# Adding DMAs for half of the weights' block sums and for the residual, with a third set of Strassen's products per down column pair

## The chip, the cores and the metric

The kernel runs on one core of a Trainium2 chip. The metric is device microseconds of one execution, the median of several runs. The engines named below are TensorE (PE), VectorE (DVE), ScalarE (ACT), GpSimd (POOL) and SyncE (SP); SP issues the loads, POOL issues a few other transfers, and both kinds run on the core's 16 DMA engines.

## The reference

A decoder layer on 256 tokens with a model width of 2048, all in float32: a half-step SwiGLU FFN, a mixer (attention with a sliding window beside a convolution module), and a second half-step FFN, each followed by LayerNorm of `ALPHA * x + sublayer(x)`. The change touches the two FFNs alone:

```python
D_MODEL, SEQ, D_FF = 2048, 256, 5632

def swiglu_ffn(x, w_gate, w_up, w_down):
    h = jax.nn.silu(x @ w_gate) * (x @ w_up)
    return h @ w_down

x = layer_norm(DEEPNORM_ALPHA * x + 0.5 * swiglu_ffn(x, ffn1_w_gate[l], ffn1_w_up[l], ffn1_w_down[l]), ln1_g[l], ln1_b[l])
...
x = layer_norm(DEEPNORM_ALPHA * x + 0.5 * swiglu_ffn(x, ffn2_w_gate[l], ffn2_w_up[l], ffn2_w_down[l]), ln3_g[l], ln3_b[l])
```

## The kernel before

**Numbers in two parts.** Each float32 weight block is split into a high part (a cast on ScalarE, line 153 or 236) and a low part (a subtraction on VectorE, line 157 or 239); so is the activation. A product is three matmuls: high by high, low by high, high by low (`mm3`, lines 624 to 626), each with a 128 x 128 stationary block and 512 moving columns.

**Strassen's sets.** The up and the down projections take their work in sets. A set is two blocks of the contraction by two column blocks of the weights by the two blocks of 128 tokens. A plain set ("C") makes eight products from two loaded pieces of 128 x 1024. A Strassen set ("S") makes seven from the same two pieces: it forms four sums of weight blocks, and on the other side four sums of activation blocks (`block_sums`). Its products 1, 5, 6 and 7 gather in PSUM banks that belong to several outputs; `shared` combines them with VectorE into four tiles `tmp`, after the last S of a pass (`by_sums`, `final`). The other banks are added by `out` when the last set ends. The eight banks fill PSUM, so the next pass can start a bank only when it has been emptied.

**Passes.** An FFN has 5632 hidden units in three parts of 16, 16 and 12 blocks of 128 (`PARTS`). For each part the up projections run in pairs of groups (`pair`), eight sets each in the order of `UP`, two of them S; then the down projection runs (`down_by_sums`), for two pairs of 512-wide column blocks, eight sets each by the string in `KINDS`. The third part has no S in the down projection and runs through `tokens_by`. In `down_by_sums` the four `tmp` tiles are added to the residual `xt` on VectorE (`plus`, line 885), queued in `st.soon`, and the other banks are added by line 881.

**The planner.** `Steps` issues the splits ahead of their use. `sources` lists the pieces in order of use. `load` keeps up to four load slots (`RAW_BUFS`) filled by DMAs of SP; an S takes one slot and one tile `rawx` of a second pool, and at most two S are open. `jobs` holds what is loaded and not yet split; `ahead` and `pace` run jobs while the block is less than seven ahead of the one in use (`LEAD`) and the eight buffers (`RING`) last. `pace` counts the time of a product against an estimated backlog of VectorE. The low part of a job is put off in `pending` until the next job. For an S, `zeroth` splits the first piece, `first` forms two sums (line 171) and splits them, `second` forms and splits a third block, `third` the fourth.

**The turn of the hidden units.** After a pair of groups, `turn` transposes the gated result on VectorE (`hr`, line 963) and sends it through DRAM by POOL: four DMAs `far` (line 968) and one `hf` (line 970), issued at once. Six steps later `split` makes the high and low blocks `hh` and `hl` for the down projection, seven for a set of kind S and four for C. A step is one call of `st.step`: two in each set, one for each piece in `tokens_by`. All engines run their instructions in the order written.

Of the kernel before, what the change touches and what calls it, by code (L numbers as in the profile page):

```python
# [9 lines left out]
F32 = mybir.dt.float32  # L10
# [4 lines left out]
ALU = mybir.AluOpType  # L15
# [3 lines left out]
P = 128  # L19
# [3 lines left out]
KT = D // P  # L23
JT = DFF // P
PARTS = ((0, 16), (16, 32), (32, 44))
KINDS = ("SCCSCCCC", "SCCSCCCC", None)
BLOCKS = {"S": 7, "C": 4}
UP = (
    ((2, "C"), (3, "C"), (0, "S"), (4, "C"), (1, "S"), (5, "C"), (6, "C"), (7, "C")),
# [23 lines left out]
BC = 6  # L53
# [21 lines left out]
class Steps:  # L75
# [6 lines left out]
    def __init__(self, nc, pool, sources, head, pooled, xT, x_raw, xcat):  # L82
        self.nc, self.pool, self.sources, self.head, self.pooled = nc, pool, sources, head, pooled
        self.xT, self.x_raw, self.xcat = xT, x_raw, xcat
        self.loaded = self.open = self.whole = self.done = self.used = self.now = 0
        self.jobs, self.ready, self.pending, self.sets = [], {}, [], 0
        self.later, self.background, self.backlog = [], None, 0.0
        self.paced, self.soon = False, []
        self.most = len(sources)

        n = KT // 2
        self.order = [g * n + t for t in range(TURNS) for g in range(2)]
        self.order += [g * n + t for g in range(2) for t in range(TURNS, n)]
# [13 lines left out]
    def raw(self):  # L107
# [2 lines left out]
        self.open += 1  # L110
        return self.pool.tile([P, 1024], F32, tag="raw", name=f"raw{n}", bufs=RAW_BUFS)

    def load(self):
        while self.open < RAW_BUFS and self.loaded < len(self.sources):
            n = self.loaded
            if isinstance(self.sources[n], tuple):
                if self.sets == 2:
                    return
                self.load_set(n)
                continue  # L120
            if n < 4:

                raws = [self.raw(), self.raw()]
                self.get_x(n, 2)
                for q in range(2):
                    for i in range(2):
                        self.get(raws[i], n + i, q * 512, 512)
                self.jobs += [("free", None, None)] * 2
                continue
            raw = self.raw()  # L130
            if n < len(self.order) and self.order[n] < KT // 2:
                self.get_x(2 * self.order[n], 2)
            self.get(raw, n, 0, 1024)
            self.jobs.append(("free", None, None))

    def load_set(self, n):

        raws = [self.raw(), self.extra.tile([P, 1024], F32, tag="rawx", name=f"rawx{n}", bufs=2)]
        self.sets += 1
        self.loaded += 3  # L140
        for raw, src in zip(raws, self.sources[n][0]):
            self.nc.sync.dma_start(raw, src)
        for i, work in enumerate((self.zeroth, self.first, self.second, self.third)):
            self.jobs.append((n + i, raws, work))

    def upper(self, n, raw):

# [19 lines left out]
            self.pending.pop(0)()  # L167
            most -= 1

    def sub(self, out, a, b):  # L170
        self.nc.vector.tensor_tensor(out=out, in0=a, in1=b, op=ALU.subtract)  # L171
        self.vector(0.6)

    def zeroth(self, n, raws):
        zero = self.upper(n, raws[0])
        self.flush()
        raws.append(zero)

    def first(self, n, raws):
        a, b = ([r[:, :512], r[:, 512:]] for r in raws[:2])  # L180
        t = [self.act.tile([P, 512], F32, tag="bc", name=f"sum{n}", bufs=BC) for _ in range(2)]
        raws.append(t)
        self.sub(t[0], b[0], a[0])
        self.sub(t[1], b[1], t[0])
        self.pending = [raws[2], self.upper(n, t)]

    def second(self, n, raws):
        b = [raws[1][:, :512], raws[1][:, 512:]]
        self.sub(b[0], b[1], b[0])
        self.pending.append(self.upper(n, raws[1]))  # L190
        self.flush(1)

    def third(self, n, raws):
        a1 = raws[0][:, 512:]
        self.sub(a1, a1, raws[3][1])
        three = self.upper(n, a1)
        self.flush(1)

        def ended():
            three()  # L200
            self.open -= 1
            self.sets -= 1
            self.load()

        self.pending.append(ended)

    def split(self):
        nc = self.nc
# [121 lines left out]
def hybrid_layer(  # L330
# [3 lines left out]
    nc = tc.nc  # L334
# [530 lines left out]
    def down_by_sums(hh, hl, kinds, factor):  # L865

        firsts = [sum(BLOCKS[k] for k in kinds[:t]) for t in range(len(kinds))]
        places = {
            "S": ("11", "22", "12", "S1", "S2", "S3", "S4"),
            "C": ("21", "11", "22", "12"),  # L870
        }

        def blocks(t, name):
            n = firsts[t] + places[kinds[t]].index(name)
            return hh[:, n], hl[:, n]

        for c in range(0, NC_, 2):
            ys = {(i, j): xt[:, 1 - i, (c + j) * 512 : (c + j + 1) * 512] for i in range(2) for j in range(2)}

            def add(out, ps, other):  # L880
                nc.vector.scalar_tensor_tensor(out=out, in0=ps, scalar=factor, in1=other, op0=ALU.mult, op1=ALU.add)
                st.vector(0.62, 0.3)

            def plus(y, t):
                nc.vector.tensor_tensor(out=y, in0=y, in1=t, op=ALU.add)
                st.vector(0.6)

            def shared(bank, ys=ys):

                tmp = [act.tile([P, 512], F32, tag="z", name="part", bufs=ZB) for k in range(4)]  # L890
                nc.scalar.mul(tmp[0], bank[1], factor)
                add(tmp[1], bank[6], tmp[0])
                add(tmp[3], bank[5], tmp[1])
                add(ys[1, 1], bank[5], ys[1, 1])
                add(tmp[2], bank[7], tmp[1])
                for n, (at, k) in enumerate((((0, 0), 0), ((0, 1), 3), ((1, 0), 2), ((1, 1), 2))):
                    st.soon.append(lambda y=ys[at], t=tmp[k]: plus(y, t))

            by_sums(kinds, blocks, lambda at, ps, ys=ys: add(ys[at], ps, ys[at]), shared)

    def ffn(xc, tag, skew, begun, prepare, finish, kept=None):
        with tc.tile_pool(name=f"ffn{tag}", bufs=2) as pool:
# [17 lines left out]
            def block_sums(out, x_):  # L920

                for o, y, z, op in (
                    (out[:, 0], x_[0], x_[2], ALU.add), (out[:, 2], x_[1], x_[0], ALU.subtract),
                    (out[:, 1], out[:, 0], x_[1], ALU.subtract), (out[:, 3], x_[3], out[:, 1], ALU.subtract),
                ):
                    nc.vector.tensor_tensor(out=o, in0=y, in1=z, op=op)
                    st.vector(0.2)
# [8 lines left out]
            for part, ((j0, j1), kinds) in enumerate(zip(PARTS, KINDS)):  # L936
                n = j1 - j0
# [22 lines left out]
                def turn(g, ht, hh=hh, hl=hl, kinds=kinds):  # L960
# [3 lines left out]
                    st.vector(1.25)  # L964
                    far = dram.tile([4, 32, 4, 2 * P], F32, tag="far", name="far")

                    for t in range(4):
                        nc.gpsimd.dma_start(far[:, :, t].rearrange("f r n -> r f n"), hr[32 * t : 32 * t + 32])  # L968
                    hf = pool.tile([P, 8 * P], F32, tag="ht", name="hf")
                    nc.gpsimd.dma_start(hf, far.rearrange("f r t n -> (f r) (t n)"))  # L970

                    def parted(at, src):
                        hi, lo = (x_[:, at : at + src.shape[1]] for x_ in (hh, hl))
# [18 lines left out]
                        parted(at, some[:, 1:])  # L992
                        parted(at + 3, sums)

                    st.at(6, lambda: st.soon.extend([lambda t=t: split(hf, t) for t in range(2)]))

                def pair(g, ups):

                    tmp, places = [], {(0, 0): 0, (0, 1): 2, (1, 0): 1, (1, 1): 3}

                    def add(out, ps, other):
                        nc.vector.tensor_tensor(out=out, in0=ps, in1=other, op=ALU.add)  # L1002
                        st.vector(0.62, 0.3)

                    def shared(bank):

                        tmp.extend(act.tile([P, 512], F32, tag="z", name="part", bufs=ZB) for k in range(4))
                        nc.scalar.copy(tmp[0], bank[1])
                        add(tmp[1], bank[6], tmp[0])
                        add(tmp[2], bank[5], tmp[1])  # L1010
                        add(tmp[1], bank[7], tmp[1])
                        add(tmp[3], bank[5], tmp[1])

                    def out(at, ps):

                        y = tmp[places[at]]
                        add(y, ps, y)
                        nc.scalar.activation(y[:, : JG * P], y[:, : JG * P], AF.Silu)

                    def gates():  # L1020
                        for at, k in places.items():
                            gate(g + at[1], 1 - at[0], tmp[k], tmp[k][:, : JG * P])
                        turn((g - j0 // JG) // 2, gated.pop())

                    by_sums("".join(kind for _, kind in ups), lambda n, name: up_blocks(ups[n][0], name), out, shared)
                    st.at(1, gates)
# [471 lines left out]
```

## Time and profile before

| | us |
|---|---|
| median of 3 runs | 1687.98 |
| lowest and highest | 1686.88, 1688.58 |
| the profiled execution | 1688.99 |
| its span | 1687.2 |

The span runs from the first to the last instruction that the profiler records. The profile's groups give count, busy time, the mean of one instruction in ns, and the engine's idle time just before them with what ended most of it. The lines themselves stand in the prediction.

### The profile page before, as it was taken

To read this page: it belongs to the slowest core of one execution; us is meant where nothing else is said; L and a number is where in the kernel's file an instruction comes from. 1 tells how busy PE (TensorE), PEld (TensorE's weight loads), DVE (VectorE), ACT (ScalarE), POOL (GpSimd) and SP (SyncE) were. 2 spreads that over 40 slices of the span, in tenths; PEclk is the share of its full clock that TensorE was granted. 3 is DMA by queue.
4 is the path that set the end of the run, shared out by engine and by line. 5 is a ranking of instruction groups with operands and counts; after the bars stand their busy time and mean duration, and the time that the engine had idled before them with its cause. 6 is when DMAs were issued, how large, how long until landed. Compare 5 with 4: busy or idle time off the path is not lost.

```text
span 1687.2 us, 21755 instructions
## 1 busy us (share of the span) xinstructions
PE 1669.7 (99%) x7689; PEld 1383.6 (82%) x7689; DVE 1386.7 (82%) x2035; ACT 912.9 (54%) x1252; POOL 268.1 (16%) x226
## 2 busy tenths in 40 slices
PE   9999999999999999999999999999999999999997
PEld 7887788888888888888888888877888888888886
DVE  7888898789888886758887778998888888988866
ACT  6556555555555554576665465555545555545541
POOL 0100000000000000178996200000000000000000
PEclk9999999999999999999999999999999999999999
DMA  8767666567666667556654555776656665666682
GB/s 295 241 211 271 219 209 218 191 223 244 214 215 211 212 213 246 171 182 194 200 181 157 198 193 196 246 236 210 219 200 215 221 237 202 222 200 224 209 279 99
DMA packets 103694, 359.47 MB, mean 213 GB/s; under 512 B 12960, under 2 KB 13088, under 8 KB 103328
## 3 DMA queue, kind: packets, MB, share of 16 engines
q1 hardware_dynamic: 96048, 334.74, 58.6%
q0 software_dynamic: 7392, 23.08, 4.5%
q8 instruction: 60, 0.98, 0.2%
q14 instruction: 50, 0.41, 0.1%
q10 hardware_dynamic: 144, 0.26, 0.0%
HBM read 344.40 MB, written 13.63 MB: 212 GB/s over the span
## 4 chain that ended last, share of the span: by engine, by line
PE 67%; DVE 19%; DMA 6%; issue 5%; ACT 3%; DVEq 0%; POOL 0%; ACTq 0%; SPq 0%; POOLq 0%
PE sum L624 13%; PE sum L625 13%; PE sum L626 13%; DVE lo L157 9%; PE acc L624 4%; PE acc L626 4%; PE acc L625 4%; DMA raw<-in_wu 3%; ACT hi L153 2%; DVE part L1002 2%; DVE sum L171 2%; PE in_c L1149 2%; PE in_a L1149 2%; PE in_q L1149 1%; DMA raw<-in_wd 1%
## 5 line engine op out<-in xcount | busy, mean ns | idle before, releaser
L157 DVE TENSOR_TENSOR lo<-raw,hi 128x1024 fp32r<-128x1024 f32 x452 | 506.6, 1153 | 121.5 <-ACT hi L153 121.0
L153 ACT CAST hi<-raw 128x1024 fp32r<-128x1024 f32 x452 | 432.9, 996 | 298.9 <-DMA raw<-in_wu 108.1
L624 PE MATMUL sum<-hi,xcat 128*128 128x512 f32 x1080 | 420.4, 389 | 1.6 <-DVE part L1002 1.6
L625 PE MATMUL sum<-lo,xcat 128*128 128x512 f32 x1080 | 420.3, 389 | 0.6 <-DVE lo L157 0.6
L626 PE MATMUL sum<-hi,xcat 128*128 128x512 f32 x1080 | 420.2, 389 | 0.0
L624 PEld LDWEIGHTS sum<-hi,xcat 128*128 128x128 f32 x1080 | 202.7, 188 | 44.7 <-DVE part L1002 2.5
L625 PEld LDWEIGHTS sum<-lo,xcat 128*128 128x128 f32 x1080 | 202.7, 188 | 42.9 <-DVE lo L157 1.0
L626 PEld LDWEIGHTS sum<-hi,xcat 128*128 128x128 f32 x1080 | 202.7, 188 | 42.2
L968 POOL DMA_DIRECT2D far<-hr x88 | 48.8, 556 | 1167.3 <-DVE hr L963 1120.9
L236 ACT CAST hi<-raw 128x1024 fp32r<-128x1024 f32 (+1 forms) x164 | 166.6, 1030 | 119.9 <-PE acc L626 71.8
L624 PE MATMUL sum<-hi,hh 128*128 128x512 f32 x496 | 194.0, 391 | 1.9 <-DVE part L1002 1.3
L239 POOL TENSOR_TENSOR lo<-raw,hi 128x1024 fp32r<-128x1024 f32 x73 | 175.6, 2423 | 117.5 <-ACT hi L236 110.6
L626 PE MATMUL sum<-hi,hl 128*128 128x512 f32 x496 | 193.1, 389 | 0.0
L625 PE MATMUL sum<-lo,hh 128*128 128x512 f32 x496 | 193.0, 389 | 0.0
L153 ACT CAST hi<-sum 128x512 fp32r<-128x512 f32 x112 | 69.5, 622 | 139.1 <-DVE sum L171 128.9
L239 DVE TENSOR_TENSOR lo<-raw,hi 128x1024 fp32r<-128x1024 f32 (+1 forms) x91 | 106.9, 1203 | 37.9 <-ACT hi L236 37.1
L1002 DVE TENSOR_TENSOR part<-sum,part 128x512 f32<-128x512 f32 x160 | 105.1, 685 | 12.7 <-PE sum L626 8.1
L624 PEld LDWEIGHTS sum<-hi,hh 128*128 128x128 f32 x496 | 93.1, 188 | 25.1 <-DVE part L1002 3.5
L626 PEld LDWEIGHTS sum<-hi,hl 128*128 128x128 f32 x496 | 93.1, 188 | 19.4
L625 PEld LDWEIGHTS sum<-lo,hh 128*128 128x128 f32 x496 | 93.1, 188 | 18.8
L1212 DVE SCALAR_TENSOR_TENSOR conv<-hc,cw_sb,conv 128x256 f32<-128x256 f32 x231 | 96.6, 482 | 1.1
L153 ACT CAST hi<-rawx 128x1024 fp32r<-128x1024 f32 x56 | 59.0, 1053 | 48.9 <-DVE rawx L171 39.3
(198 smaller groups left out, 2319.2 us busy)
## 6 DMA issues: line engine op xcount, KB each, us to landing
raw<-in_wu SPq DMA_DIRECT2D x308, 512.0 KB, 4.8
raw<-in_wd SPq DMA_DIRECT2D x160, 512.0 KB, 4.7
raw<-in_win SPq DMA_DIRECT2D x52, 512.0 KB, 4.1
rawx<-in_wu SPq DMA_DIRECT2D x40, 512.0 KB, 6.3
raw<-in_wout SPq DMA_DIRECT2D x32, 512.0 KB, 3.7
far<-hr POOLq DMA_DIRECT2D x88, 128.0 KB, 2.7
hf<-far POOLq DMA_DIRECT2D x22, 512.0 KB, 3.6
rawx<-in_wd SPq DMA_DIRECT2D x16, 512.0 KB, 6.4
```

The costliest lines, as they stand in the source:

```text
L153: self.nc.scalar.copy(hi, x_)
L157: self.nc.vector.tensor_tensor(out=lo, in0=x_, in1=hi.bitcast(F32), op=ALU.subtract)
L171: self.nc.vector.tensor_tensor(out=out, in0=a, in1=b, op=ALU.subtract)
L236: nc.scalar.copy(hi, raw)
L239: eng.tensor_tensor(out=lo, in0=raw, in1=hi.bitcast(F32), op=ALU.subtract)
L624: nc.tensor.matmul(ps, s_hi, m_hi, start=start, stop=False)
L625: nc.tensor.matmul(ps, s_hi, m_lo, start=False, stop=False)
L626: nc.tensor.matmul(ps, s_lo, m_hi, start=False, stop=stop)
L968: nc.gpsimd.dma_start(far[:, :, t].rearrange("f r n -> r f n"), hr[32 * t : 32 * t + 32])
L1002: nc.vector.tensor_tensor(out=out, in0=ps, in1=other, op=ALU.add)
L1149: nc.tensor.matmul(ps, w[0][:, n], x1[:, k], start=k == 0, stop=False)
L1212: nc.vector.scalar_tensor_tensor(out=out, in0=x_, scalar=w, in1=acc, op0=ALU.mult, op1=ALU.add)
```

## The change

`KINDS` becomes `SCCSCSCC` in two parts of each FFN, so each pass of the down projection has three S. Of the four block sums of an S, VectorE forms two (`sums`, both into tiles of the pool `bc`); the other two are made in place by DMAs that add, issued by POOL. `sums` is put in the list of jobs before the piece that was loaded ahead of the set, and `third` is held until the next piece is loaded. The four `tmp` tiles of the down projection are added to the residual by adding DMAs. Signs are turned so that only additions are needed. The DMAs `far` and `hf` are issued one and three steps after the transpose, and the split follows at step 7 instead of 6.

```diff
-KINDS = ("SCCSCCCC", "SCCSCCCC", None)
+KINDS = ("SCCSCSCC", "SCCSCSCC", None)
...
+    def last_third(self):
+        if self.held is not None:
+            self.jobs.append(self.held)
+            self.held = None
...
     def load_set(self, n):
...
-        for i, work in enumerate((self.zeroth, self.first, self.second, self.third)):
+        early = len(self.jobs) > 3 and self.jobs[-1][0] == "free"
+        at = len(self.jobs) - 2 if early else len(self.jobs)
+        self.jobs.insert(at, (n - early, raws, self.sums))
+        for i, work in enumerate((self.zeroth, self.first, self.second)):
             self.jobs.append((n + i, raws, work))
+        self.held = (n + 3, raws, self.third)
...
+    def sums(self, n, raws):
+        a, b = ([r[:, :512], r[:, 512:]] for r in raws[:2])
+        t = [self.act.tile([P, 512], F32, tag="bc", name=f"sum{n}", bufs=BC) for _ in range(2)]
+        raws.append(t)
+        self.plus(t[0], a[0], b[0])
+        self.plus(t[1], t[0], b[1])
+        self.nc.gpsimd.dma_start(b[0], b[1], accum_op=ALU.add)
 
     def zeroth(self, n, raws):
         zero = self.upper(n, raws[0])
         self.flush()
-        raws.append(zero)
+
+        def ended():
+            zero()
+            self.nc.gpsimd.dma_start(raws[0][:, 512:], raws[2][1], accum_op=ALU.add)
+
+        self.pending = [ended]
 
     def first(self, n, raws):
-        a, b = ([r[:, :512], r[:, 512:]] for r in raws[:2])
-        t = [self.act.tile([P, 512], F32, tag="bc", name=f"sum{n}", bufs=BC) for _ in range(2)]
-        raws.append(t)
-        self.sub(t[0], b[0], a[0])
-        self.sub(t[1], b[1], t[0])
-        self.pending = [raws[2], self.upper(n, t)]
+        one = self.upper(n, raws[2])
+        self.flush()
+        self.pending = [one]
 
     def second(self, n, raws):
-        b = [raws[1][:, :512], raws[1][:, 512:]]
-        self.sub(b[0], b[1], b[0])
-        self.pending.append(self.upper(n, raws[1]))
-        self.flush(1)
+        two = self.upper(n, raws[1])
+        self.flush()
+        self.pending = [two]
 
     def third(self, n, raws):
-        a1 = raws[0][:, 512:]
-        self.sub(a1, a1, raws[3][1])
-        three = self.upper(n, a1)
-        self.flush(1)
+        three = self.upper(n, raws[0][:, 512:])
+        self.flush()
...
                 nc.scalar.mul(tmp[0], bank[1], factor)
                 add(tmp[1], bank[6], tmp[0])
-                add(tmp[3], bank[5], tmp[1])
-                add(ys[1, 1], bank[5], ys[1, 1])
+                add(tmp[3], bank[5], tmp[1], ALU.subtract)
                 add(tmp[2], bank[7], tmp[1])
-                for n, (at, k) in enumerate((((0, 0), 0), ((0, 1), 3), ((1, 0), 2), ((1, 1), 2))):
-                    st.soon.append(lambda y=ys[at], t=tmp[k]: plus(y, t))
+                add(tmp[1], bank[5], tmp[2], ALU.subtract)
+                for at, k in ((0, 0), 0), ((0, 1), 3), ((1, 0), 2), ((1, 1), 1):
+                    nc.gpsimd.dma_start(ys[at], tmp[k], accum_op=ALU.add)
...
-                    for t in range(4):
-                        nc.gpsimd.dma_start(far[:, :, t].rearrange("f r n -> r f n"), hr[32 * t : 32 * t + 32])
+                    def leave():
+                        for t in range(4):
+                            nc.gpsimd.dma_start(far[:, :, t].rearrange("f r n -> r f n"), hr[32 * t : 32 * t + 32])
+
                     hf = pool.tile([P, 8 * P], F32, tag="ht", name="hf")
-                    nc.gpsimd.dma_start(hf, far.rearrange("f r t n -> (f r) (t n)"))
+                    st.at(1, leave, True)
+                    st.at(3, lambda: nc.gpsimd.dma_start(hf, far.rearrange("f r t n -> (f r) (t n)")), True)
...
-                    st.at(6, lambda: st.soon.extend([lambda t=t: split(hf, t) for t in range(2)]))
+                    st.at(7, lambda: st.soon.extend([lambda t=t: split(hf, t) for t in range(2)]))
```

More of the change, by code (lines that the diff above doesn't have):

```diff
@@ L111, in raw @@
         return self.pool.tile([P, 1024], F32, tag="raw", name=f"raw{n}", bufs=RAW_BUFS)
+    def last_third(self):
+        if self.held is not None:
+            self.jobs.append(self.held)
+            self.held = None
     def load(self):
@@ L118, in load @@
                     return
+                self.last_third()
                 self.load_set(n)
@@ L134, in load @@
             self.jobs.append(("free", None, None))
+            self.last_third()
     def load_set(self, n):
@@ L168, in flush, with plus @@
             most -= 1
-    def sub(self, out, a, b):
-        self.nc.vector.tensor_tensor(out=out, in0=a, in1=b, op=ALU.subtract)
+    def plus(self, out, a, b):
+        self.nc.vector.tensor_tensor(out=out, in0=a, in1=b, op=ALU.add)
         self.vector(0.6)
+    def sums(self, n, raws):
[5 more added lines that the diff above has]
+        self.nc.gpsimd.dma_start(b[0], b[1], accum_op=ALU.add)
     def zeroth(self, n, raws):
@@ L878, in down_by_sums, with add @@
             ys = {(i, j): xt[:, 1 - i, (c + j) * 512 : (c + j + 1) * 512] for i in range(2) for j in range(2)}
-            def add(out, ps, other):
-                nc.vector.scalar_tensor_tensor(out=out, in0=ps, scalar=factor, in1=other, op0=ALU.mult, op1=ALU.add)
+            def add(out, ps, other, op=ALU.add):
+                nc.vector.scalar_tensor_tensor(out=out, in0=ps, scalar=factor, in1=other, op0=ALU.mult, op1=op)
                 st.vector(0.62, 0.3)
-            def plus(y, t):
-                nc.vector.tensor_tensor(out=y, in0=y, in1=t, op=ALU.add)
-                st.vector(0.6)
             def shared(bank, ys=ys):
@@ L922, in block_sums @@
                 for o, y, z, op in (
-                    (out[:, 0], x_[0], x_[2], ALU.add), (out[:, 2], x_[1], x_[0], ALU.subtract),
-                    (out[:, 1], out[:, 0], x_[1], ALU.subtract), (out[:, 3], x_[3], out[:, 1], ALU.subtract),
+                    (out[:, 0], x_[0], x_[2], ALU.subtract), (out[:, 2], x_[1], x_[0], ALU.subtract),
+                    (out[:, 1], out[:, 0], x_[1], ALU.subtract), (out[:, 3], x_[3], out[:, 1], ALU.add),
                 ):
@@ L993, in split, with add @@
                         parted(at + 3, sums)
-                    st.at(6, lambda: st.soon.extend([lambda t=t: split(hf, t) for t in range(2)]))
+                    st.at(7, lambda: st.soon.extend([lambda t=t: split(hf, t) for t in range(2)]))
                 def pair(g, ups):
                     tmp, places = [], {(0, 0): 0, (0, 1): 2, (1, 0): 1, (1, 1): 3}
-                    def add(out, ps, other):
-                        nc.vector.tensor_tensor(out=out, in0=ps, in1=other, op=ALU.add)
+                    def add(out, ps, other, op=ALU.add):
+                        nc.vector.tensor_tensor(out=out, in0=ps, in1=other, op=op)
                         st.vector(0.62, 0.3)
@@ L1009, in shared @@
                         add(tmp[1], bank[6], tmp[0])
-                        add(tmp[2], bank[5], tmp[1])
+                        add(tmp[2], bank[5], tmp[1], ALU.subtract)
                         add(tmp[1], bank[7], tmp[1])
-                        add(tmp[3], bank[5], tmp[1])
+                        add(tmp[3], bank[5], tmp[1], ALU.subtract)
                     def out(at, ps):
```

2 lines of the change are left out of this document (1 added, 1 removed).

## The prediction

> **What bounds the kernel now.** I read the page's head and its chain of waits first, then the busy time of TensorE in stretches, then TensorE's timeline row by row, then VectorE's groups with the shapes kept apart, and last the transfers.
>
> ```profile
> span 1687.2 us, 21755 instructions
> PE 1669.7 (99%) x7689; PEld 1383.6 (82%) x7689; DVE 1386.7 (82%) x2035; ACT 912.9 (54%) x1252; POOL 268.1 (16%) x226
> PE 67%; DVE 19%; DMA 6%; issue 5%; ACT 3%; DVEq 0%; POOL 0%; ACTq 0%; SPq 0%; POOLq 0%
> ```
>
> TensorE is all but full, VectorE has about a fifth free, and the chain still runs through VectorE for 19% of the span: weights are sometimes ready only just in time. A busy TensorE need not be at its peak pace, so I count its matmuls in stretches (columns: stretch, length, busy time with count, clock, DMA share, GB/s) and look at single starts (start, duration).
>
> ```profile
> 100.00:200.00 100.00, 98.55 (x431) 1.00 0.68 237
> 200.00:300.00 100.00, 99.87 (x441) 1.00 0.63 213
> 300.00:400.00 100.00, 100.00 (x443) 1.00 0.66 222
> 1000.00:1100.00 100.00, 99.42 (x439) 1.00 0.63 217
> 1100.00:1200.00 100.00, 97.72 (x425) 1.00 0.67 226
> ```
>
> ```profile
> 121.32 0.39 PE L624 MATMUL sum<-hi,xcat 128*128 128x512 f32 x1
> ...
> 134.24 0.39 PE L624 MATMUL sum<-hi,xs 128*128 128x512 f32 x1
> ...
> 1101.67 0.39 PE L626 MATMUL sum<-hi,xs 128*128 128x512 f32 x1
> 1102.95 0.50 PE L624 MATMUL sum<-hi,xcat 128*128 128x512 f32 x1 [0.89 <-DVE part L1002]
> ```
>
> From 121.32 to 134.24 lie 19 products of three matmuls: 12.92 / 57 = 0.227 us from start to start. The 389 ns shown for one matmul overlap its neighbours and are not what one costs. At this pace 100 us hold 443, as in 300 to 400. The other four stretches lack 12, 2, 4 and 18, so 36 starts or 8.2 us are lost there, although three of them look 98 to 100% busy. The pair at 1101.67 shows how: the next start comes 1.28 us later instead of 0.23, since VectorE's adds (L1002) had not yet emptied the bank. Ahead of such a place in FFN 1 the chain reads (start, length):
>
> ```profile
> 152.04 4.13 DMA raw<-in_wu
> ...
> 161.32 6.95 DMA rawx<-in_wd
> ...
> 179.87 2.40 DVE part L1002 x4
> ```
>
> Late transfers made VectorE late, and VectorE is too full to catch up at once.
>
> **The products.** Each FFN has two parts with Strassen's products in the down projection, each runs two column pairs: 8 passes. Each pass gets one more set S (7 products) for a set C (8). That is 8 products or 24 matmuls, 24 x 0.227 = **5.4 us** less on the engine that is full. The same two 512 KB blocks are loaded by S and by C, so no weight traffic is added. The Trainium skill (TensorE: Matmul & The Clock Gate, Back-to-back issue gap) gives about 131 ns as the sustained spacing of such matmuls, by which 24 would be 3.1 us; this trace has 0.227 us, and that decides.
>
> **VectorE.**
>
> ```profile
> L157 DVE TENSOR_TENSOR lo<-raw,hi 128x1024 fp32r<-128x1024 f32 x396 | 470.9, 1219 | 112.3 <-ACT hi L153 111.7
> L1002 DVE TENSOR_TENSOR part<-sum,part 128x512 f32<-128x512 f32 x160 | 105.1, 685 | 12.7 <-PE sum L626 8.1 <-ACT part L1008 2.0
> L157 DVE TENSOR_TENSOR lo<-sum,hi 128x512 fp32r<-128x512 f32 x112 | 72.0, 683 | 0.0
> L171 DVE TENSOR_TENSOR sum<-rawx,sum 128x512 f32<-128x512 f32 x56 | 38.8, 692 | 1.9
> L171 DVE TENSOR_TENSOR raw<-raw,sum 128x512 f32<-128x512 f32 x56 | 38.4, 685 | 0.8
> L157 DVE TENSOR_TENSOR lo<-raw,hi 128x512 fp32r<-128x512 f32 x56 | 38.3, 685 | 9.3 <-ACT hi L153 9.3
> L171 DVE TENSOR_TENSOR rawx<-rawx 128x512 f32<-128x512 f32 x56 | 38.3, 684 | 0.0
> L171 DVE TENSOR_TENSOR sum<-rawx,raw 128x512 f32<-128x512 f32 x56 | 37.8, 675 | 11.7 <-DMA rawx<-in_wd 7.1 <-DMA rawx<-in_wu 4.5
> L949 DVE TENSOR_TENSOR ht<-part 128x256 f32<-128x256 f32 x80 | 28.5, 417 | 0.0
> L963 DVE STREAM_TRANSPOSE hr<-ht 128x1024 f32<-128x1024 f32 x22 | 27.4, 1245 | 0.7
> L885 DVE TENSOR_TENSOR xt<-xt,part 128x512 f32<-128x512 f32 x32 | 19.9, 682 | 0.0
> ```
>
> Two of a set's four block sums go to DMAs: 56 x (0.684 + 0.685) = 76.7 us. The 32 additions to the residual (L885) go too: 32 x 0.682 = 21.8. An S cost VectorE four sums (2.74), two wide lows (2.44) and three narrow ones (2.05), 7.22 us; with two sums it is 5.86. A C costs 2.44. Eight added sets bring 8 x 3.42 = 27.4 us, and the four added splits of the hidden units into seven blocks an estimated 4 x 2.5 = 10 (four small sums and one more low, at 0.69 for 512 columns, with a start for each). Net about 61 us of 1386.7 go.
>
> By stage: an up pair is 186 matmuls or 42.2 us of TensorE. VectorE's share of it was 2 x 7.22 + 6 x 2.44 + 8 x 0.685 + 4 x 0.417 + 1.25 + about 1.4 of splits = 38.9, and becomes 36.2. A down pair had 2 x 7.22 + 6 x 2.44 + 12 adds of 0.68 = 37.2 of 42.2, and gets 3 x 5.86 + 5 x 2.44 + 8 x 0.68 = 35.2 of 41.5. So about 6 us are free in either. ScalarE gets twelve wide casts more in all and is 54% busy: nothing.
>
> What is the relief worth? Between nothing and the 8.2 us lost above. Those stretches start with transfers, which the change makes more of, so I take a quarter: **2 us**.
>
> **The adding DMAs.** No row shows one. There are 2 x 64 for sets and 8 x 4 for the residual, 160 of 256 KB. The nearest rows (issue to landing in us) and the waits for the sets' second half:
>
> ```profile
> far<-hr POOLq DMA_DIRECT2D x88, 128.0 KB, 2.7
> hf<-far POOLq DMA_DIRECT2D x22, 512.0 KB, 3.6
> rawx<-in_wd SPq DMA_DIRECT2D x16, 512.0 KB, 6.4
> L968 POOL DMA_DIRECT2D far<-hr x88: 550/551/747, 55.9 to 1617.0; - x88
> q0 software_dynamic: 7392, 23.08, 4.5%
> DVE sum L171 <- DMA rawx<-in_wd: 7.1, 6, 1.4
> DVE sum L171 <- DMA rawx<-in_wu: 4.5, 7, 1.2
> ```
>
> Landing lies between 2.7 and 6.4; I take 3.6, since reading source and target moves 512 KB. POOL spends 160 x 0.55 = 88 us on issues in stages where it is idle. On the engines 41.9 MB at q0's rate are 8%, twice that if the target counts again, over the share of 0.63 to 0.68 in the stretches above.
>
> **The waits this adds.** (1) The third block's DMA starts after the first sum. ScalarE's cast of that block stops all casts behind it until it lands, then its low stops VectorE. Between the first sum and this low VectorE has 0.69 + 3 lows of 1.22, 1.22 and 1.37 = 4.5 us to do; with landing L the block's high is ready at L + 1.05. So VectorE loses L - 3.5 a set: 0.1 at 3.6, nothing against 6 us free. (2) The sums stand up to two lows (2.44 us) earlier in VectorE's queue, so VectorE, and the lows behind, may wait for the 6.4 us landing of rawx. It waited 13 times in 56 before. At most 2.44 a set: 4.9 of 6 free in an up pair, 7.3 of 6.3 in a down pair, so 0 to 8 us; I take 0, as the weights run up to seven blocks ahead. The load slot of a set is also held one block longer; the same lead covers it, and without it each such load is one 2.4 us job late. (3) The last adds of a pass wait for the residual's DMAs. From `shared` to the first of them are 12 products, 8.2 us; the four tmp adds take 2.7, the scaling 0.6, an issue 0.55 and landing 3.6: 7.5, so hidden. If late, the bank is next needed 8 products (5.4 us) on. (4) `far` and `hf` are issued some steps later, so POOL's queue is free for the adding DMAs instead of waiting on a transpose. Their reader moves from step 6 to 7. In the up stages steps of 2.4 us or more remain. In the last part of FFN 2 it is close:
>
> ```profile
> 1628.56 1.14 ACT L976 CAST hh<-hf 128x512 fp32r<-128x512 f32 x2 [1.57 <-DMA hf<-far]
> 1629.21 1.29 DVE L977 TENSOR_TENSOR hl<-hf,hh 128x512 fp32r<-128x512 f32 x2 [0.96 <-ACT hh L976]
> 1631.62 0.39 PE L624 MATMUL acc<-hi,hh 128*128 128x512 f32 x1
> ```
>
> The first half is ready at 1629.9 and needed at 1631.6; one more cast and low (1.0 and 1.2 us) ahead of it cost 0 to 1.2 us. I take **0.3**.
>
> **Sum.** -5.4 - 2.0 + 0.3 = -7.1. The profiled execution took 1688.99 us, 1.8 more than its span; 1681.9 would follow, and as the median of the runs shown is 1.0 lower, **1680.9**.
>
> **Rivals.** *All the relief*: VectorE, 3 to 6% freer in each stage, is never late. For: the late adds are its own. Against: transfers start the lateness. -5.4 - 8.2 gives 1674.4. *New waits eat it*: wait (2) in full, 8 us in the down pairs, with the products' 5.4: 1690.6; at half, 1686.6. For: VectorE already waited for rawx. Against: all weights run ahead. *Slower*: landing of the adding DMAs. The point is where a down pair's three waits pass its 6.3 us: 3 x (L - 3.5) = 6.3, L = 5.6. At the 6.4 of rawx, 3 x 2.9 - 6.3 = 2.4 us in each of 8 pairs, 19 - 5.4 = +14: 1702. For: those are loads of like traffic. Against: POOL's own queue shows 2.7 and 3.6. *Starved issues*: POOL, writing the descriptors, waits out two wide lows of VectorE at each issue, 2.4 us; that is L = 6.0 and by the same count 3 x 2.5 - 6.3 = 1.2 in each of 8 pairs, 10 - 5.4 = +4.6: 1692.6. Against: 88 issues beside such lows took 550 to 747 ns. The Trainium skill (SBUF — State Buffer, SBUF: two separate sides) says that a VectorE operation holding the ports shared with GpSimd keeps it from writing descriptors, 3100 ns instead of 620; by that rule the slow issues would be seen here, and the trace of before does not show them.
>
> **How the numbers follow.** Forecast and its neighbours (1677 to 1684) 0.50; all the relief 0.14; new waits 0.22, mostly inside 0.2%; slower by landing 0.11; starved issues 0.03. A measurement of this kernel tells 0.2% or 3.4 us from no change. Faster takes the first two and 0.02 of the third: 0.66; same 0.18; slower 0.02 + 0.14 = 0.16. The range 1675 to 1689 leaves out the slower cases and the tip of the relief, under 0.2.
>
> **What would show it.** Right: TensorE at 443 in each stretch of 100 us, 24 matmuls fewer; L885 gone; L171 two to a set; adding DMAs landing under 5 us; 61 us less VectorE. Wrong: TensorE waits on lows or on the last adds in the down pairs; idle before the casts put down to an adding DMA; long waits of the sums for rawx.

## The result, and the profile after

The changed kernel takes 1809.51 us (median of 4 runs, 1808.03 to 1811.1) against 1688.28 us before: a ratio of 1.0718, with a 95% interval of 1.0699 to 1.0736. It is slower by 121 us, where 1680.9 us was forecast.

The head of the page of the changed kernel, and its chain of waits:

```profile
span 1806.7 us, 22167 instructions
PE 1708.4 (95%) x7665; PEld 1395.4 (77%) x7665; DVE 1333.8 (74%) x1951; ACT 917.9 (51%) x1280; POOL 410.2 (23%) x386
PE 40%; DMA 27%; DVE 18%; issue 7%; ACT 4%; POOL 2%; SPq 1%; DVEq 0%; ACTq 0%; POOLq 0%
```

TensorE runs 24 matmuls fewer (7665 instead of 7689), and VectorE has 53 us less to do, as it should be. Still the span is 119.5 us longer. TensorE's idle time, span less busy time, went from 17.5 to 98.3 us: 80.8 us. Its busy time grew by 38.7 us although there is less work: after each wait a matmul stands alone in the record with 0.39 us or more instead of the 0.227 that it costs in a full row, and some ran at a lower clock. The chain went from 6% on transfers to 27%.

The stretches of TensorE (length, busy time with count, granted clock, DMA share, GB/s), first by 100 us and then inside one of the worst:

```profile
200.00:300.00 100.00, 87.68 (x361) 0.92 0.83 231
300.00:400.00 100.00, 100.00 (x434) 0.98 0.76 225
500.00:600.00 100.00, 87.27 (x357) 0.93 0.79 219
```

```profile
220.00:240.00 20.00, 18.97 (x82) 1.00 0.81 223
240.00:260.00 20.00, 14.47 (x48) 0.74 0.87 244
260.00:280.00 20.00, 20.00 (x90) 1.00 0.66 198
```

200 to 300 and 500 to 600 are for the most part down projections of FFN 1. They start 361 and 357 matmuls where a full stretch has 443. The second fence shows where slower matmuls come from: from 240 to 260 TensorE is granted 0.74 of its clock, so 48 matmuls in 14.47 busy us take 0.30 us each, not 0.227. Inside it the clock falls to 0.50 after a wait, so there the wait is paid a second time in slow matmuls. Here are that place and another, each with the start of the matmul that waited (in brackets how long) and a short stretch behind it:

```profile
241.72 0.50 PE L643 MATMUL sum<-hi,hh 128*128 128x512 f32 x1 [2.26 <-DVE xt L900]
244.00:246.00 2.00, 0.77 (x2) 0.50 1.00 311
1220.27 0.50 PE L643 MATMUL sum<-hi,hh 128*128 128x512 f32 x1 [3.20 <-DVE part L1020]
1220.00:1222.00 2.00, 1.65 (x6) 1.00 0.97 358
```

The Trainium skill (TensorE: Matmul & The Clock Gate, HAM oscillation — how this bites in real kernels) states that gaps of more than about 3.4 us throttle the clock. In this trace the clock also fell behind a wait of 2.26 us, and it stayed at 1.00 behind one of 3.20 us, so the length of one wait does not decide it alone.

Who waited for whom in the changed kernel (us in total, times, longest):

```profile
ACT hi L165 <- DMA raw<-sum: 214.0, 58, 7.8
ACT hi L165 <- DMA rawx<-rawx: 142.2, 60, 7.4
DVE sum L183 <- DMA rawx<-in_wu: 55.1, 27, 5.1
DVE sum L183 <- DMA rawx<-in_wd: 27.2, 13, 5.2
PE sum L643 <- DVE xt L900: 49.5, 22, 4.6
DVE xt L900 <- DMA xt<-part: 36.7, 16, 4.4
```

Nearly every set (58 and 60 of 64) makes ScalarE wait twice, for the fourth block's sum (`raw<-sum`, 3.7 us each) and for the third's (`rawx<-rawx`, 2.4 us). The sums on VectorE wait for their load 40 times in 64; before it was 13 in 56. One set in the timeline, ScalarE's rows and then POOL's (start, duration, in brackets the idle time ahead and what ended it):

```profile
329.57 1.05 ACT L165 CAST hi<-rawx 128x1024 fp32r<-128x1024 f32 x1 [2.74 <-DMA rawx<-rawx]
330.52 1.05 ACT L165 CAST hi<-raw 128x1024 fp32r<-128x1024 f32 x1
334.83 1.57 ACT L165 CAST hi<-raw 128x512 fp32r<-128x512 f32 x2 [3.25 <-DMA raw<-sum]
```

```profile
325.86 0.86 POOL L192 DMA_DIRECT2D rawx<-rawx  x1 [20.61 <-DVE sum L183]
329.99 0.86 POOL L200 DMA_DIRECT2D raw<-sum  x1 [3.27 <-DVE lo L169]
```

The second adding DMA could not be issued before 329.99, because it overwrites what the zeroth block's low reads, and that low stands behind two others on VectorE. It lands 4.8 us later. By then ScalarE has run one cast and waited 3.25 us, with all later casts queued behind. The adding DMAs' issues and landings (median us):

```profile
rawx<-rawx POOLq DMA_DIRECT2D x64, 256.0 KB, 3.6
raw<-sum POOLq DMA_DIRECT2D x64, 256.0 KB, 4.4
xt<-part POOLq DMA_DIRECT2D x32, 256.0 KB, 4.7
q0 software_dynamic: 30432, 65.03, 18.5%
```

Landing is what I had taken, 3.6, for the third block; for the fourth block and the residual it is about 1 us longer. POOL's queue went from 4.5 to 18.5% of the DMA engines for 41.9 MB more, some 14 points, which lies between the 8 and the 16 that were worked out. The loads did not land later for it: the medians of `raw<-in_wu` and `raw<-in_wd` are 4.6 and 4.7 us here, and 4.8 and 4.7 before.

### The profile page after: what moved, and what is told of

The parts are those of the page before. It is cut to its first block, busy times and chain, and to the rows that moved or that the text cites. A ratio compares the mean times of both kernels' runs of the same rounds, so it can differ in the third digit from the quotient of the medians.

```text
span 1806.7 us, 22167 instructions
## 1 busy us (share of the span) xinstructions
PE 1708.4 (95%) x7665; PEld 1395.4 (77%) x7665; DVE 1333.8 (74%) x1951; ACT 917.9 (51%) x1280; POOL 410.2 (23%) x386
## 3 DMA queue, kind: packets, MB, share of 16 engines
q1 hardware_dynamic: 96048, 334.74, 54.9%
q0 software_dynamic: 30432, 65.03, 18.5%
## 4 chain that ended last, share of the span: by engine, by line
PE 40%; DMA 27%; DVE 18%; issue 7%; ACT 4%; POOL 2%; SPq 1%; DVEq 0%; ACTq 0%; POOLq 0%
DVE lo L169 9%; DMA raw<-sum 6%; PE sum L643 6%; PE sum L644 6%; PE sum L645 6%; DMA rawx<-in_wu 5%; DMA rawx<-in_wd 5%; PE acc L645 3%; PE acc L643 3%; PE acc L644 3%; DMA raw<-in_wu 3%; ACT hi L165 3%; DMA xt<-part 2%; DMA rawx<-rawx 2%; PE in_c L1167 2%
## 5 line engine op out<-in xcount | busy, mean ns | idle before, releaser
L169 DVE TENSOR_TENSOR lo<-raw,hi 128x1024 fp32r<-128x1024 f32 (+1 forms) x452 | 503.9, 1144 | 182.4 <-ACT hi L165 181.6
L165 ACT CAST hi<-raw 128x1024 fp32r<-128x1024 f32 (+1 forms) x452 | 428.5, 986 | 395.4 <-DMA raw<-sum 214.0
L643 PE MATMUL sum<-hi,xcat 128*128 128x512 f32 x1080 | 426.4, 395 | 25.8 <-DVE part L1020 14.0
L644 PE MATMUL sum<-lo,xcat 128*128 128x512 f32 x1080 | 425.0, 394 | 3.3 <-DVE lo L169 3.2
L645 PE MATMUL sum<-hi,xcat 128*128 128x512 f32 x1080 | 424.0, 393 | 0.0
L643 PEld LDWEIGHTS sum<-hi,xcat 128*128 128x128 f32 x1080 | 205.4, 190 | 76.7 <-DVE part L1020 16.5
L192 POOL DMA_DIRECT2D rawx<-rawx x64 | 55.8, 872 | 845.3 <-DVE sum L183 827.7
L645 PEld LDWEIGHTS sum<-hi,xcat 128*128 128x128 f32 x1080 | 204.8, 190 | 42.8
L643 PE MATMUL sum<-hi,hh 128*128 128x512 f32 x488 | 199.0, 408 | 38.5 <-DVE xt L900 24.7
L255 ACT CAST hi<-raw 128x1024 fp32r<-128x1024 f32 (+1 forms) x164 | 166.3, 1030 | 119.9 <-PE acc L645 59.6
L165 ACT CAST hi<-rawx 128x1024 fp32r<-128x1024 f32 x64 | 67.4, 1053 | 154.6 <-DMA rawx<-rawx 142.2
L258 DVE TENSOR_TENSOR lo<-raw,hi 128x1024 fp32r<-128x1024 f32 (+1 forms) x91 | 106.3, 1195 | 39.2 <-ACT hi L255 38.4
L183 DVE TENSOR_TENSOR sum<-raw,rawx 128x512 f32<-128x512 f32 x64 | 44.1, 690 | 82.3 <-DMA rawx<-in_wu 55.1
L169 DVE TENSOR_TENSOR lo<-rawx,hi 128x1024 fp32r<-128x1024 f32 x64 | 78.1, 1220 | 34.0 <-ACT hi L165 34.0
```

Source lines behind the costliest of these rows:

```text
L165: self.nc.scalar.copy(hi, x_)
L169: self.nc.vector.tensor_tensor(out=lo, in0=x_, in1=hi.bitcast(F32), op=ALU.subtract)
L183: self.nc.vector.tensor_tensor(out=out, in0=a, in1=b, op=ALU.add)
L192: self.nc.gpsimd.dma_start(b[0], b[1], accum_op=ALU.add)
L255: nc.scalar.copy(hi, raw)
L258: eng.tensor_tensor(out=lo, in0=raw, in1=hi.bitcast(F32), op=ALU.subtract)
```

## The experiments

The medians of the kernel before beside these runs were 1687.1 to 1688.9 us. Where a ratio is given the run was timed in rounds; the others are single runs. "Slots" are the load slots, `RAW_BUFS`.

### First round: which part of the change

**Residual back on VectorE** (e1)

```diff
-                    nc.gpsimd.dma_start(ys[at], tmp[k], accum_op=ALU.add)
+                    st.soon.append(lambda y=ys[at], t=tmp[k]: plus(y, t))
```

> The changed kernel with the 32 additions to the residual back on VectorE; the weights' sums still by DMA, three sets. Theory W (ScalarE's casts wait for the weights' adding DMAs, 356 us of waits in the trace, and VectorE behind them): little comes back, at most 45 us of the 121, about 1770 to 1800 us. Rival R (the last adds of a down pass wait for the residual's DMAs, and TensorE for the banks; 54.6 us of TensorE's lost time follows L900): 55 us and the slow clock after it come back, about 1720 to 1750 us.

1810.9 us: nothing came back, less than either theory wanted. TensorE's waits moved from the last adds (49.5 us in the changed kernel, 8.0 here) to lows that come late (3.9 there, 31.6 here). As long as casts are late anyway, the residual's DMAs cost nothing more. The mean clock was higher here, 0.983 against 0.974, at the same time, so over the whole run the slow matmuls are not simply added on top.

**Block sums back on VectorE, old order of jobs** (e2)

```diff
-        self.plus(t[0], a[0], b[0])
-        self.plus(t[1], t[0], b[1])
-        self.nc.gpsimd.dma_start(b[0], b[1], accum_op=ALU.add)
...
+        self.plus(b[0], b[0], b[1])
+        self.pending.append(self.upper(n, raws[1]))
+        self.flush(1)
...
+        self.plus(a1, a1, raws[3][1])
```

> The changed kernel with the two block sums back on VectorE in the old order of jobs; the residual still by DMA, three sets. Theory W: most comes back, 1690 to 1720 us, casts wait for no adding DMA. Rival R: the end of each down pass stays late, 1750 us or more.

1716.9 us: 92.6 us of the 121 came back with this part of the change, as theory W has it. But 30 us of loss stayed.

**Third set alone** (e3)

```diff
-KINDS = ("SCCSCCCC", "SCCSCCCC", None)
+KINDS = ("SCCSCSCC", "SCCSCSCC", None)
```

> The kernel before with the third set alone, all sums and additions on VectorE. By the products alone 5.4 us faster than before, 1682.6. Rival S (the third set asks more of VectorE than a pass has: 3 x 7.22 + 5 x 2.44 + 12 x 0.68 = 42.0 us of 41.5): at least 8 x 0.5 = 4 us lost again and lateness as in the early pairs, 1684 to 1695.

1750.4 us, ratio 1.0365 (1.0347 to 1.0382): 63 us slower, far outside what either case allowed. The one term of the prediction that seemed safe, 24 matmuls fewer, loses 63 us by itself. VectorE is not full: the deficit that I had counted is 0.5 us a pass, the loss is 8. This opened the question that the second round is about. The run above (e2, 1716.9) has the same three sets with the block sums on VectorE too, and is 33 us faster than this one; it differs by the residual's DMAs, by the signs and by the later turn of the hidden units, which no run takes apart.

**Two sets, all else as changed** (e4)

```diff
-KINDS = ("SCCSCSCC", "SCCSCSCC", None)
+KINDS = ("SCCSCCCC", "SCCSCCCC", None)
```

> The changed kernel with two sets per pass, so all that is done by DMA stays but the last S lies four C instead of two ahead of the last adds. Theory W: 16 of 128 sums' DMAs fewer, about an eighth of the loss comes back, 1790 to 1800. Rival R: the residual's DMAs get 21.8 us instead of 10.9 to land, so 55 us and more come back, 1730 to 1750. Rival S: nearly all comes back.

1786.4 us: 23 us came back, between the ranges of the theories. On top of the adding DMAs the third set costs less than alone, so the parts do not add up. That they strain one thing is a guess here, which the second round tries.

### Second round: what the parts have in common

A piece's way is: its load waits for a slot, takes about 5 us, is cast, its low is made, and the slot is free. Before, there are four slots, and SP's queue waited 884 us for lows to free them:

```profile
SPq L104 <- DVE lo L157: 884.1, 338, 10.7
```

So theory L: with four slots the supply is bound by this loop and not by any engine's busy time, and each wait inside the loop is paid in full, since the idle time of VectorE behind it cannot be used.

**Third set alone, five slots** (e9)

```diff
-RAW_BUFS = 4
+RAW_BUFS = 5
-BC = 6
+BC = 5
...
-            pT = pool.tile([P, 2, 3 * P], F32, tag="pT", name="pT", bufs=2)
+            pT = pool.tile([P, 2, 3 * P], F32, tag="pT", name="pT", bufs=1)
```

> The kernel before with the third set alone, all on VectorE (1750.4 with four load slots), now with five load slots; the room comes from one buffer fewer for the chunks and for the attention's transposed shares. Theory L (in a set the supply is bound by the loop of load, cast, low and slot, not by VectorE's sum of work): most of the 63 us comes back, 1685 to 1710. Rival S (VectorE's work of 42.0 us in a pass of 41.5): little comes back, 1735 to 1755.

1687.4 us, ratio 0.9992 (0.9982 to 1.0001): all 63 us came back. Against its own control, the kernel before with the same five slots (e11 below, 1684.2), the third set still costs 3 us where it should gain 5.4. The casts' waits for loads, with four slots and then with five:

```profile
ACT hi L153 <- DMA raw<-in_wu: 147.2, 63, 5.0
ACT hi L153 <- DMA raw<-in_wd: 62.6, 35, 3.6
```

```profile
ACT hi L153 <- DMA raw<-in_wu: 43.6, 40, 4.9
ACT hi L153 <- DMA raw<-in_wd: 13.4, 11, 2.7
```

The loads themselves landed a little later than with four slots (5.2 us against 4.9), and still the casts waited 153 us less. SP's own waits for slots hardly tell the two apart. With five slots they are

```profile
SPq L104 <- DVE lo L157: 619.3, 321, 11.0
SPq L142 <- DVE lo L157: 354.8, 58, 14.1
```

which is 974 us, against 1036 with four; the kernel before, which loses little, has 968. So the queue of loads waits for slots with the loss and without it, and it is the casts' waits for loads that show the difference.

**Idle traffic** (e8)

```diff
+        for _ in range(2):
+            self.nc.gpsimd.dma_start(self.spare[0], self.spare[1], accum_op=ALU.add)
```

> The kernel before with two adding DMAs of 256 KB in each set on tiles that nothing else uses, 112 in all: the traffic without a wait; its results are unchanged. Theory W: the loads land a little later, at most 10 us more, 1688 to 1698. Rival T (the traffic itself makes the loads late; the DMA share rises by about 10 points): 40 us or more, above 1727.

1730.4 us, ratio 1.0251 (1.0236 to 1.0266): 42 us for 112 DMAs that no cast waits for. That is the rival's number. VectorE was no busier (1386.2 us). The loads landed half a us later, and the casts waited 265 us for them instead of 191. Before:

```profile
raw<-in_wu SPq DMA_DIRECT2D x308, 512.0 KB, 4.8
```

```profile
ACT hi L153 <- DMA raw<-in_wu: 110.5, 48, 5.0
ACT hi L153 <- DMA raw<-in_wd: 81.0, 49, 4.6
```

With the idle traffic:

```profile
raw<-in_wu SPq DMA_DIRECT2D x308, 512.0 KB, 5.3
raw<-in_wd SPq DMA_DIRECT2D x160, 512.0 KB, 5.3
```

```profile
ACT hi L153 <- DMA raw<-in_wu: 164.6, 60, 7.0
ACT hi L153 <- DMA raw<-in_wd: 100.6, 51, 6.9
```

Whether that is the traffic as such or the loop again was tried with five slots (e20, the same edit and `RAW_BUFS = 5`, `BC = 4`):

> The same control with the idle traffic of 112 adding DMAs (42 us slower with four slots). Theory L: the later landing of the loads is hidden by the fifth slot, at most 8 us above the control. Rival T (traffic costs by itself): 30 us or more above it.

1684.8 us, ratio 0.9978 (0.9969 to 0.9987), 5 us above its control of 1679.7 (e19, below), although the loads now took longer still:

```profile
raw<-in_wu SPq DMA_DIRECT2D x308, 512.0 KB, 5.5
raw<-in_wd SPq DMA_DIRECT2D x160, 512.0 KB, 5.7
```

With four slots the same traffic costs 42 us, with five it costs 5: it acts through the loop. These 42 us cannot simply be taken as a part of the changed kernel's 121, since there the loads land no later than before.

**Order of jobs, all sums on VectorE** (e5)

```diff
-        self.nc.gpsimd.dma_start(b[0], b[1], accum_op=ALU.add)
...
-            self.nc.gpsimd.dma_start(raws[0][:, 512:], raws[2][1], accum_op=ALU.add)
...
+        self.plus(raws[1][:, :512], raws[1][:, :512], raws[1][:, 512:])
         two = self.upper(n, raws[1])
...
+        self.plus(raws[0][:, 512:], raws[0][:, 512:], raws[2][1])
         three = self.upper(n, raws[0][:, 512:])
```

> The changed kernel with all four block sums on VectorE, but in the changed order of jobs (two sums one piece earlier, the fourth block one piece later). It differs from the run with the old order (1716.9) by the order alone, and from the changed kernel (1809.5) by the 128 adding DMAs alone. Theory W (the landing of the adding DMAs, with casts queued behind it): 1705 to 1730. Rival O (the order: sums that wait for the second piece's load, and a load slot held for one more piece): 1770 or more.

1783.8 us, the rival's number, but the trace names another cause than the rival. The cast of the third block now waits for its sum on VectorE, which stands behind the lows of the blocks before it. The same wait in this run, and in the run with the old order, where the sum stands ahead of the lows that are put off:

```profile
ACT hi L165 <- DVE rawx L183: 247.3, 54, 7.3
```

```profile
ACT hi L161 <- DVE rawx L179: 60.7, 23, 3.5
```

So this run does not single out the order; it has a wait of 4.6 us at the same place as the adding DMA's. That it does not matter what the cast waits for is suggested, not shown: the early sums also wait 136 us for the load of the second piece here, and 36 us in the run with the old order.

**Third block alone by DMA** (e6: the fourth's sum as in e5, the third's by DMA)

> The changed kernel with the third block's sum by DMA and the fourth's on VectorE: one adding DMA a set instead of two. Theory W: each of the two waits has its part (214 us of ScalarE's waits for the fourth block, 142 us for the third), so between: 1745 to 1775. If one of the two holds the pipeline alone: below 1730 or above 1790.

1786.4 us, outside the ranges expected: with one wait for a DMA or with one for VectorE the loss is much the same, and the second DMA adds 23 us to get to the changed kernel.

**Fourth block not held** (e13: e5 with the edit below)

```diff
-        self.held = (n + 3, raws, self.third)
+        self.jobs.append((n + 3, raws, self.third))
```

> Four slots; the run with the changed order and all sums on VectorE (1783.8), but the fourth block no longer held for the next piece. If the held slot makes the loss of the order (theory L): 1720 to 1745. If the sums that stand one piece earlier make it (VectorE waits for the second piece's load, 136 us in that trace): 1765 to 1785.

1787.0 us: the held slot is not what costs. My own theory lost here. The rival, that the early sums' wait for the load makes the loss (144 us of such waits in this run), came within 2 us of its range. No run has the sums on VectorE, in the new order but not early, so that rival stays open for this kernel.

**Sums not early** (e14: the changed kernel with the edit below)

```diff
-        early = len(self.jobs) > 3 and self.jobs[-1][0] == "free"
+        early = False
```

> The changed kernel (four slots, three sets) with the two sums directly ahead of their set instead of one piece earlier. Theory W: the adding DMAs get less time to land, so 1810 to 1850, slower than the change. Rival O (VectorE waits 82 us for the second piece's load because the sums stand early): 1760 to 1795.

1836.6 us, 27 us slower than the change, as theory W has it: the early sums pay, though VectorE waits for the load. Without them the casts wait longer for the third block's DMA (252 us against 142) and for the two sums (120 against 32), and hardly at all for the fourth block's (6 against 214). These three waits in sum are no longer than in the change (378 us against 388), so the sum of waits alone does not give the time.

**No cast waits** (e18: e4 with the edit below, which leaves out the sums of the third and fourth blocks)

```diff
-        self.nc.gpsimd.dma_start(b[0], b[1], accum_op=ALU.add)
+        self.nc.gpsimd.dma_start(self.spare[0], self.spare[2], accum_op=ALU.add)
...
-            self.nc.gpsimd.dma_start(raws[0][:, 512:], raws[2][1], accum_op=ALU.add)
+            self.nc.gpsimd.dma_start(self.spare[1], self.spare[2], accum_op=ALU.add)
```

> The changed kernel with two sets per pass (1786.4), the two adding DMAs of each set issued at the same places but on tiles that nothing else uses: the same order and traffic, no cast waits for them. The third and fourth block stay without their sums, so that part of the computation is left out. Theory W (waits for landing): 1700 to 1735, about the 42 us of the idle traffic at most. Rival T or O (traffic or the order of jobs): 1760 or more.

1722.6 us against 1786.4 with the waits: without them 64 us of the 99 that the two-set kernel loses come back. Order, traffic and the residual's DMAs keep the other 35, which this run does not divide. The traffic is not quite the same, as the idle DMAs landed after 7.6 us instead of 3.6 and 4.3, and the casts wait 379 us for loads here, against 125 in e4.

### Third round: the change with slots to spare

**Changed kernel, five slots** (e10, the same three edits as in e9)

> The changed kernel whole, with five load slots (the same room as in the third-set run with five). Theory L (all parts of the loss go through one loop: a slot comes free late, so its next load starts late and the casts run out of data): most of the 121 us comes back, 1685 to 1715. Rival W (the casts wait for the adding DMAs themselves, whatever the slots): 1740 or more.

1749.8 us, ratio 1.0361 (1.0344 to 1.0379): half of the loss came back, and 61 us did not, more than theory L gave; the number is in the rival's range. The casts still waited 319 us for the adding DMAs, against 356 with four slots. So the slots are half of the account; e15 and e12 below show where the other half lies. The worst stretches lie in the down passes, where TensorE waited for the last adds:

```profile
PE sum L643 <- DVE xt L900: 34.2, 14, 4.5
```

**The same, residual on VectorE** (e15, e10 with e1's edit)

> The changed kernel with five slots (1749.8), the additions to the residual back on VectorE. With four slots this changed nothing (1810.9). Rival R (with slots to spare, the last adds of a pass wait for the residual's DMAs: TensorE's lost time after them is 37 of 69 us): 1700 to 1725. Theory W (the sums' DMAs keep the down passes late): 1735 or more.

1724.5 us, 25 us better: in the rival's range. 36 us above the kernel before remain, and the casts still wait 341 us for the sums' DMAs. What cost nothing with four slots (e1) costs 25 with five, and TensorE's wait is now

```profile
PE sum L643 <- DVE xt L900: 5.8, 6, 1.0
```

**Old order, residual by DMA, five slots** (e12, e2 with the three edits)

> Five load slots, three sets, block sums on VectorE in the old order, the residual by DMA (1716.9 with four slots). Theory L: 1680 to 1692, within 5 us of the third set alone with five slots; the residual's DMAs are then neither here nor there. Rival R: the end of each pass still waits for them, 1695 or more.

1683.1 us, ratio 0.9966 (0.9954 to 0.9979). Between this and e10 lie only the adding DMAs for the sums and their order: 67 us, with five slots too; no run divides the two there. With the sums on VectorE the residual's DMAs do no harm: TensorE waits 1.0 us for the last adds, where it waited 34.2 us in e10.

**Kernel before, five slots** (e11, the three edits)

> The kernel before with five load slots: the control for the two runs with five. Theory L: its 8 us of TensorE's lost time go, and the smaller room in the mixer gives some of it back: 1680 to 1690. If five slots with three sets (1687.4) carry the 5.4 us of the products, this run is some 5 us above that, 1692; if the smaller room costs nothing, it is 1680.

1684.2 us, ratio 0.9973 (0.9963 to 0.9984): TensorE's loss in the FFNs is gone, and the mixer's smaller room gives some back.

**The room taken elsewhere**: e12 (e17) and the kernel before (e19), both with `RAW_BUFS = 5` and `BC = 4` and the mixer untouched

> Five load slots, three sets, sums on VectorE in the old order, residual by DMA, as the run at 1683.1, with the room taken from the chunks' buffers alone (four instead of six) and the mixer as before. If the mixer's smaller room cost some 4 us there (the control lost 1.2 us of TensorE's time in the FFNs instead of 9.5, but gained only 4.2): 1677 to 1681. If two buffers fewer hold the sums or the residual's chunks up: 1683 or more.

> The kernel before with five load slots and four chunk buffers: the control for the best version (1678.9). Theory L: TensorE's lost time of 8 us goes, 1678 to 1682. If the third set's 24 matmuls come through in the best version, this run is 3 to 5 us above it, 1682 to 1684; if they do not, it is level with it.

The first took 1678.9 us, ratio 0.9942 (0.9929 to 0.9956); the second 1679.7, ratio 0.9949 (0.9936 to 0.9963). Both beat the change, and the kernel before by half a percent, and they cannot be told apart: the gain is the fifth slot's. FFN 2's first part in the one with three sets, and then in the other:

```profile
1100.00:1200.00 100.00, 98.39 (x428) 1.00 0.70 231
```

```profile
1100.00:1200.00 100.00, 100.00 (x443) 1.00 0.66 229
```

15 starts or 3.4 us are lost there with three sets, of the 5.4 us that the matmuls save; the medians differ by 0.8, and the other 1.2 us were not traced.

## Why the prediction was wrong

Two steps failed: VectorE's idle time was counted as free, some 6 us in each pair, and the fourth block's adding DMA, on which the casts then waited longest, was given no term. Term by term:

**The products.** Right in size as far as TensorE goes: 24 matmuls fewer. "The same two 512 KB blocks are loaded by S and by C, so no weight traffic is added" is true (334.74 MB in both), but it was taken as if nothing else changed for the supply. A set holds its slot for four jobs where a piece holds it for one. That this is what fills the loop is argued from the code; that the loss goes through the slots is shown by e3 and e9 with its control (63 us with four slots, 3 with five). In no run did the 5.4 us come in full.

**VectorE.** The sum of work was well sized: 61 us less foretold, 52.9 measured. What failed is the sentence "So about 6 us are free in either", and all that was paid out of it. VectorE's idle time before was not free to spend: idle traffic that made the loads land half a us later cost 42 us with four slots (e8) and 5 with five (e20), with VectorE no busier. That its idle time lay in the loop, behind loads that could not start earlier, is how I read these runs; no run shows it directly. The size of the failure can be estimated by the prediction's own count. VectorE's idle time before the early sums and before the lows of the third and fourth blocks grew by 2.95 us a set (from the sums' waits for their load and from the lows' rows under Wait (1)). By the count of 6 and 6.3 us free, that would cost nothing in an up pair and 2.6 us in a down pair, some 20 us in eight. About 127 are missing, the products' 5.4 included.

**The relief.** 2 us were taken for a freer VectorE. The 8.2 us that were to be had did not hang on VectorE's work: with five slots the four stretches that lacked 36 starts hold 443 each, with VectorE as busy as before (e11, 1390.5 us). The row that pointed there was the casts' 191 us of waits for loads, which I did not use for a term.

**Wait (1).** "nothing against 6 us free": for the third block landing was as taken, 3.6, and VectorE's own loss was small as forecast, though ScalarE waited 2.4 us a set. The fourth block's DMA had no term at all, and that is the term that was missing. It can only be issued after a low, and its cast follows two casts later; the casts waited 214 us for it. VectorE's lows of the third block before, and of the third and the fourth after, with the idle time ahead of them at the end (for the fourth before, the prediction shows 9.3):

```profile
L157 DVE TENSOR_TENSOR lo<-rawx,hi 128x1024 fp32r<-128x1024 f32 x56 | 68.3, 1219 | 13.8 <-ACT hi L153 13.7
L169 DVE TENSOR_TENSOR lo<-rawx,hi 128x1024 fp32r<-128x1024 f32 x64 | 78.1, 1220 | 34.0 <-ACT hi L165 34.0
L169 DVE TENSOR_TENSOR lo<-raw,hi 128x512 fp32r<-128x512 f32 x64 | 44.2, 691 | 112.4 <-ACT hi L165 112.3
```

e18 puts both waits at 64 of 99 us with two sets.

**Wait (2).** Bounded at 0 to 8 us and taken as nothing, "as the weights run up to seven blocks ahead". VectorE did wait, 82 us in 40 sets. But with adding DMAs the early place as a whole is a gain of 27 us (e14).

**Wait (3).** "7.5, so hidden". The residual's DMAs landed in 4.7 instead of 3.6 us and took 0.945 us to issue (30.3 us for 32) instead of 0.55. The cover of 8.2 us was short 16 times. With the supply late they cost nothing more (e1), with five slots 25 us (e10 against e15).

**Wait (4)** was not singled out by any run; the step of 0.3 us stays open.

**The rivals.** "Slower" had the right sign, but by luck: its condition, a landing above 5.6 us, did not come about (medians of 3.6 to 4.7), and its point stood on the 6 us of slack. "Starved issues" did not come about either: no issue of an adding DMA took longer than 1.23 us. No rival had the slots, the fourth block's DMA, or a clock that falls after a wait.

## What to carry to other kernels

Idle time on an engine is slack only if the engine has work it could do then: ask first whether the stream that feeds it is bound by buffers (here casts that waited for loads while the queue of loads waited for slots), and try one buffer more before anything that takes work off the engine. Work moved to a DMA is not gone but becomes latency, and where an in-order queue reaches its reader before it lands, everything behind the reader waits too. A DMA that replaces 0.7 us of an engine's work and takes 4 us to land would need its reader moved by those 4 us, and its issue not tied to a late instruction; no run here tried that.

## What the runs showed of the hardware that was not expected

An adding DMA uses the DMA engines about twice as long as a load of its size. In the changed kernel the loads' queue stands so (packets, MB, share of the 16 engines over the span; POOL's, `q0`, is shown with the result):

```profile
q1 hardware_dynamic: 96048, 334.74, 54.9%
```

The loads' 334.74 MB took 54.9% of 1806.7 us, 337 GB/s while busy. POOL's queue took 18.5% of that span and 4.5% of 1687.2 us before, so the 41.9 MB of the adding DMAs took some 258 us, or 162 GB/s. POOL's plain transfers before, 23.08 MB in 76 us, ran at 304 GB/s, so it is not the queue as such; the adding DMAs' rows are half as long as the loads', and what that adds was not tried. The Trainium skill (Collectives: The Full Stack, The bandwidth ceiling: the fold count and why AG ≠ RS ≠ AR) states that the reduce of a collective emits two read descriptors for each chunk; the factor of two here agrees with it. POOL took 0.87 to 0.95 us on the mean to issue an adding DMA, against 0.55 to 0.57 for a plain copy.
